# PSUM banks for attention's last transposes, and the queue that loads the gates' block sums

## The chip, the cores and the metric

The kernel runs on one core of a Trainium2 chip. The metric is device time in microseconds of one execution; the profile is one execution on the same core.

## The reference

One layer of a hybrid encoder over 1024 tokens and 16 learned meta tokens, width 1024. After an RMSNorm one input projection gives the operands of two branches and two gates. Branch A is neighbourhood attention (8 heads of 64, a window of 8 x 16 grid positions, meta keys always visible), branch Bm a bidirectional gated linear recurrence (HGRN2, 4 heads of 128). Then:

```
A = neighbourhood_attention(q, k, v, rpb) @ W_na_out ;  Bm = hgrn2(q, z_f, z_b, i, g) @ W_hg_out
h = h + (sigmoid(gate_na) * A + sigmoid(gate_hg) * Bm) @ W_o
h = h + relu(rmsnorm(h) @ W_up)^2 @ W_down ;  out = rmsnorm(h)
```

Matmuls keep float32 accuracy: each operand is split into a rounded high part and a low remainder, and a product is three matmuls, high by high, high by low and low by high.

## The kernel before

The stages follow each other: norm and transpose of the input, HGRN2 for four heads, attention for four pairs of heads, the gates, the branches' output projections, W_o, and the MLP. TensorE runs nearly all the time. Outside some stages that are recorded in written order, a scheduler sets each engine's order from the program; attention and the gates are such scheduled code, and it mixes the end of the first with the start of the second.

**Attention's end.** For each strip of 128 tokens and head, `scores` (two matmuls, L756 and L757) fills one of two PSUM banks of tag `s`; VectorE adds the bias and takes a minimum, ScalarE the exponential, VectorE scales (L766). `values`, two strips behind, transposes the probabilities on TensorE (L777, L779) into one of two banks of tag `t` (tile `ppt`), which ScalarE copies as the high part (L788) and VectorE turns into the low part (L789); both must have read a bank before it is filled again. Every fourth strip, a chain of matmuls (L793 to L802, tile `pov`) applies the values; VectorE moves the result to `OT` (L804, L806), and GpSimd's queue writes `OT` to DRAM (L817).

**The gates.** The 16 blocks of gate columns are computed in pairs by a scheme with sums of blocks (Winograd's). `first_gates` makes the first product of every pair for two pairs at a time: it loads two weight blocks of 512 KB through SyncE's queue (L102), splits them (ScalarE L112 into `hi`, VectorE L113 into `lo`) and runs chains of matmuls (L836 to L838) on two banks of tag `mm`; ScalarE copies the halves out (L869, L857). The `raw`, `hi` and `lo` tiles have two buffers each. The last call, for pairs 6 and 7, takes the last two blocks. Then `gate_pair` runs once per pair, with `second_operand` ahead of it: for each of four kinds of block sums of the activations, `t2`, `t1`, `t3`, `t4`, four tiles of 256 KB that `block_sums` had written to DRAM (`tsp`) in attention are loaded into `gv` (L889, five buffers, SyncE's queue) and split (ScalarE L96, VectorE L97). A `gv` buffer comes free when both have read it; the split tiles of `t3` stand where attention's `OT` stood, and wait for its write.

The engines and both kinds of queue take their work in order: a waiting instruction holds what stands behind it.

Of the kernel before, what the change touches and what calls it, by code (L numbers as in the profile page):

```python
# [26 lines left out]
NPAIR = 4  # L27
# [21 lines left out]
def layer(ctx: ExitStack, tc: tile.TileContext, x, meta, w_in, w_na, w_hg, w_o, w_up, w_dn,  # L49
          g_mix, g_mlp, g_fin, gain, bias, lbl, lmask, wmask, out):  # L50
    nc = tc.nc
    pe, act, dve, pool, sp = nc.tensor, nc.scalar, nc.vector, nc.gpsimd, nc.sync
# [20 lines left out]
    def bank(tag, name):  # L73
        return banks[tag].tile([P, 4, P], F32, tag=tag, name=name)
# [20 lines left out]
    def split(hi, lo, src):  # L95
        act.copy(hi, src)  # L96
        dve.tensor_tensor(lo, src, hi.bitcast(F32), op=ALU.subtract)  # L97
# [82 lines left out]
    tsp = {v: [dramp.tile([P, TH], F32, name=f"tsp_{v}_{k}") for k in range(4)] for v in ("t1", "t2", "t3", "t4")}  # L180
# [491 lines left out]
    with (tc.tile_pool(name="npr", bufs=1, side="right", reuse_waits="tile") as npr,  # L672
# [18 lines left out]
        for p in range(NPAIR):  # L691
# [43 lines left out]
            for b in (0, 4, 8):  # L735
                pt = bank("t", "vpt")
# [12 lines left out]
            def scores(s, i):  # L749
                js = [j for j in (s - 1, s, s + 1) if 0 <= j < 8]  # L750
                w = len(js) * SW
                o = 432 if s == 0 else 720 if s == 7 else 0
                sc = bank("s", "nsc").rearrange("p a b -> p (a b)")
                ksl = KS[i][:, js[0]:js[-1] + 1].rearrange("p s c -> p (s c)")
                kll = KL[i][:, js[0]:js[-1] + 1].rearrange("p s c -> p (s c)")
                pe.matmul(sc[:, :w], QX[i][:, s], ksl, start=True, stop=False)  # L756
                pe.matmul(sc[:, :w], QX[i][:, s], kll, start=False, stop=True)  # L757
                pr = npr.tile([P, 432], F32, tag="pr", name="pr", bufs=5)
                mn = npr.tile([P, 1], F32, tag="mn", name="mn", bufs=4)
                sm = npr.tile([P, 1], F32, tag="sm", name="sm", bufs=4)  # L760
                rc = npr.tile([P, 1], F32, tag="rc", name="rc", bufs=4)
                dve.tensor_tensor_reduce(out=pr[:, :w], in0=sc[:, :w], in1=NB[:, i, o:o + w], scale=1.0,  # L762
                                         scalar=3.0e38, op0=ALU.add, op1=ALU.min, accum_out=mn)
                act.activation(pr[:, :w], pr[:, :w], AF.Exp, bias=mn, scale=-1.0, accum_out=sm)
                dve.reciprocal(rc, sm)
                dve.tensor_scalar(pr[:, :w], pr[:, :w], rc, None, op0=ALU.mult)  # L766
                return js, pr

            def values(s, i, js, pr):
                g, e = divmod(s, 4)  # L770
                if e == 0:
                    po[i] = [npr.tile([P, 22, P], F32R, tag=f"PT{q}", name=f"PT{q}") for q in range(2)]
                PH, PL = po[i]
                m = len(js)
                pt = bank("t", "ppt")
                for k in range(m):
                    pe.transpose(pt[:, k], pr[:, k * SW:k * SW + P], ident)  # L777
                cen = js.index(s)
                pe.transpose(pt[:, m], pr[:, cen * SW + NM:cen * SW + NM + P], ident)  # L779

                b0 = 3 * (js[0] - 4 * g) + e + 3
                if s < 7:
                    runs = [(0, m + 1, b0)]
                else:
                    runs = [(0, m, b0), (m, 1, 4 * e + 9)]
                for k, n, b in runs:
                    hi = PH[:, b:b + 3 * n - 2:3]
                    act.copy(hi, pt[:, k:k + n])  # L788
                    dve.tensor_tensor(PL[:, b:b + 3 * n - 2:3], pt[:, k:k + n], hi.bitcast(F32), op=ALU.subtract)  # L789
                if e < 3:  # L790
                    return
                ov = bank("b", "pov")
                pe.matmul(ov, V[:, 8, i], PH[:, 9:22:4], start=True, stop=False)  # L793
                for a in range(-1, 5):
                    j = 4 * g + a
                    if 0 <= j < 8:
                        es = [q for q in range(4) if abs(a - q) <= 1]
                        e0, ne = es[0], len(es)
                        b = 3 * a + e0 + 3
                        pe.matmul(ov[:, e0:e0 + ne], V[:, j, i], PH[:, b:b + ne], start=False, stop=False)  # L800
                        pe.matmul(ov[:64, e0:e0 + ne], V[:, j, i, :64], PL[:, b:b + ne], start=False, stop=False)
                pe.matmul(ov, V[:, 8, i], PL[:, 9:22:4], start=False, stop=True)  # L802
                low = npr.tile([64, 4, P], F32, tag="low", name="low")
                dve.tensor_copy(low, ov[64:])  # L804
                dst = OT[64 * i:64 * i + 64].rearrange("p (r s c) -> p s r c", s=8, c=8)
                dve.tensor_tensor(dst[:, s - 3:s + 1], ov[:64].rearrange("p s (r c) -> p s r c", c=8),  # L806
                                  low.rearrange("p s (r c) -> p s r c", c=8), op=ALU.add)
# [3 lines left out]
            for st in steps:  # L811
                pend.append((*st, *scores(*st)))
                if len(pend) > 2:
                    values(*pend.pop(0))
            for st in pend:
                values(*st)
            pool.dma_start(osp[1][p], OT)  # L817


# [61 lines left out]
    def g_tile(tag, n, dt=F32, bufs=1):  # L881
        return gp.tile([P, n], dt, tag=tag, name=tag, bufs=bufs)

    def second_operand(v):
        for k in range(4):
            t = g_tile("gv", TH, bufs=5)
            if v not in aV:
                aV[v] = [gpr.tile([P, 4, TH], F32R, name=f"a{v}{q}") for q in range(2)]
            sp.dma_start(t, tsp[v][k])  # L889
            split(aV[v][0][:, k], aV[v][1][:, k], t)  # L890

    w_turn = [0]
# [55 lines left out]
    for v in ("t2", "t1", "t3", "t4"):  # L948
        second_operand(v)
# [28 lines left out]
    for br, wsrc in enumerate((w_hg, w_na)):  # L978
        for jj in range(0, KC, 2):
# [7 lines left out]
            for j in (jj, jj + 1):  # L987
                sg = sgp.tile([P, T], F32, tag="sg", name="sg")
                sp.dma_start(sg, gsp[8 * br + j])
                for h in range(2):  # L990
                    pm = mm_tile()
                    t = slice(h * TH, (h + 1) * TH)
# [614 lines left out]
```

## Time and profile before

| | us |
|---|---|
| runs shown | 1538.90, 1539.66, 1540.40 |
| their median | 1539.66 |
| profiled execution, its own time | 1541.84 |
| its span, from the first to the last instruction | 1540.0 |

The profiled execution lies 2.18 us above the median, and its span 1.84 us below its own time. TensorE is busy for 1504.0 us of the span, VectorE for 1029.9, ScalarE for 658.6, GpSimd for 377.9. Starts are given in us from the start of the span. "PE" is TensorE, "PEld" its weight loads, "DVE" VectorE, "ACT" ScalarE, "POOL" GpSimd, "SP" SyncE; a "q" behind an engine's name is its queue. A row's bracket tells how long the engine was idle ahead of it and what ended that.

### The profile page before, as it was taken

To read this page: it belongs to the slowest core of one execution; us is meant where nothing else is said; L and a number is where in the kernel's file an instruction comes from. 1 tells how busy PE (TensorE), PEld (TensorE's weight loads), DVE (VectorE), ACT (ScalarE), POOL (GpSimd) and SP (SyncE) were. 2 spreads that over 40 slices of the span, in tenths; PEclk is the share of its full clock that TensorE was granted. 3 is DMA by queue.
4 is the path that set the end of the run, shared out by engine and by line. 5 is a ranking of instruction groups with operands and counts; after the bars stand their busy time and mean duration, and the time that the engine had idled before them with its cause. 6 is when DMAs were issued, how large, how long until landed. Compare 5 with 4: busy or idle time off the path is not lost.

```text
span 1540.0 us, 23453 instructions
## 1 busy us (share of the span) xinstructions
PE 1504.0 (98%) x9192; PEld 1253.4 (81%) x9192; DVE 1029.9 (67%) x1603; ACT 658.6 (43%) x1175; POOL 377.9 (25%) x354
## 2 busy tenths in 40 slices
PE   7899999999999998999999999999999999999998
PEld 5788888888888887888888887888888888888886
DVE  6666666664966877666566358877777544877876
ACT  6231313124665667434223135555555533434444
POOL 2313131216225310011000122444333200232142
PEclk9999999999999999999999999999999999999999
DMA  4111111113123128434747123444444676563224
GB/s 168 43 29 56 29 56 29 56 29 120 58 72 120 49 76 260 143 123 158 252 158 246 42 83 129 158 153 154 151 151 153 202 270 235 194 232 115 96 82 151
DMA packets 142449, 195.61 MB, mean 127 GB/s; under 512 B 8049, under 2 KB 90097, under 8 KB 142338
## 3 DMA queue, kind: packets, MB, share of 16 engines
q1 hardware_dynamic: 133216, 172.53, 33.8%
q10 hardware_dynamic: 6946, 14.24, 2.4%
q0 software_dynamic: 2176, 7.34, 1.3%
q8 instruction: 72, 1.18, 0.3%
q14 instruction: 39, 0.32, 0.1%
HBM read 139.56 MB, written 54.53 MB: 126 GB/s over the span
## 4 chain that ended last, share of the span: by engine, by line
PE 89%; DVE 5%; issue 2%; ACT 2%; POOL 1%; DMA 1%; POOLq 0%; ACTq 0%; DVEq 0%
PE mm L122 11%; PE mm L123 11%; PE mm L124 10%; PE mm L1329 5%; PE pa L1329 4%; PE pb L836 4%; PE pb L838 4%; PE pb L837 4%; PE pb L1329 4%; PE pc L1329 4%; PE pc L838 3%; PE pc L836 3%; PE pc L837 3%; PE pa L838 2%; PE pa L837 2%
## 5 line engine op out<-in xcount | busy, mean ns | idle before, releaser
L122 PE MATMUL mm<-aT,hi 128*128 128x512 f32 (+2 forms) x640 | 230.6, 360 | 3.1 <-DVE QX L707 1.5
L124 PE MATMUL mm<-aT,lo 128*128 128x512 f32 (+2 forms) x640 | 227.8, 356 | 0.5 <-DVE lo L113 0.5
L123 PE MATMUL mm<-aT,hi 128*128 128x512 f32 (+2 forms) x640 | 226.4, 354 | 0.0
L122 PEld LDWEIGHTS mm<-aT,hi 128*128 128x128 f32 x640 | 121.8, 190 | 17.6 <-issue 1.7
L124 PEld LDWEIGHTS mm<-aT,lo 128*128 128x128 f32 x640 | 121.8, 190 | 14.2 <-DVE lo L113 1.0
L123 PEld LDWEIGHTS mm<-aT,hi 128*128 128x128 f32 x640 | 121.8, 190 | 12.3
L97 DVE TENSOR_TENSOR dl<-ur,dh 128x1024 fp32r<-128x1024 f32 x54 | 71.0, 1315 | 87.4 <-ACT dh L96 85.4
L96 ACT CAST dh<-ur 128x1024 fp32r<-128x1024 f32 x54 | 56.8, 1052 | 166.5 <-issue 91.2
L112 ACT CAST hi<-raw 128x1024 fp32r<-128x1024 f32 x36 | 37.8, 1051 | 99.1 <-PE mm L123 68.0
L1134 DVE TENSOR_TENSOR wl<-raw,wh 128x512 fp32r<-128x512 f32 x50 | 41.0, 822 | 36.5 <-ACT wh L1133 36.4
L1138 ACT ACTIVATE uv<-uv 128x512 f32<-128x512 f32 x48 | 30.4, 633 | 80.0 <-DVE uv L1246 48.9
L1134 DVE TENSOR_TENSOR wl<-sx,wh 128x512 fp32r<-128x512 f32 x70 | 61.0, 882 | 3.4 <-ACT wh L1133 3.3
L1133 ACT CAST wh<-sx 128x512 fp32r<-128x512 f32 x70 | 42.1, 619 | 42.2 <-PE pc L837 24.0
L1419 POOL TENSOR_TENSOR w<-w,tt 128x512 f32<-128x512 f32 x16 | 23.4, 1460 | 132.9 <-DVE tt L1418 113.2
L300 POOL TENSOR_TENSOR Y<-X,TN 128x512 f32<-128x512 f32 x20 | 34.2, 1711 | 86.1 <-DVE X L297 86.1
L113 DVE TENSOR_TENSOR lo<-raw,hi 128x1024 fp32r<-128x1024 f32 x36 | 46.5, 1293 | 9.6 <-ACT hi L112 9.5
L762 DVE CUSTOM_DVE_ANT_0 pr<-nsc,NB 128x432 f32<-128x432 f32 (+1 forms) x64 | 35.2, 559 | 26.6 <-PE nsc L757 26.4
L836 PE MATMUL pb<-nt,wh 128*128 128x512 f32 x128 | 50.2, 392 | 0.4 <-DVE uv L1216 0.2
L122 PE MATMUL mm<-wh,mT 128*128 128x512 f32 x128 | 50.2, 392 | 0.0
L837 PE MATMUL pb<-nt,wh 128*128 128x512 f32 x128 | 49.9, 390 | 0.0
L838 PE MATMUL pb<-nt,wl 128*128 128x512 f32 x128 | 49.9, 390 | 0.0
L124 PE MATMUL mm<-wh,mT 128*128 128x512 f32 x128 | 49.9, 390 | 0.0
(391 smaller groups left out, 4354.0 us busy)
## 6 DMA issues: line engine op xcount, KB each, us to landing
raw<-in_w_in SPq DMA_DIRECT2D x56, 512.0 KB, 3.9
ur<-usp SPq DMA_DIRECT2D x54, 512.0 KB, 3.4
raw<-in_w_up SPq DMA_DIRECT2D x16, 1024.0 KB, 6.1
usp<-us SPq DMA_DIRECT2D x60, 256.0 KB, 2.2
sg<-gsp SPq DMA_DIRECT2D x16, 512.0 KB, 3.3
w<-in_w_dn SPq DMA_DIRECT2D x16, 512.0 KB, 4.5
usp<-uv SPq DMA_DIRECT2D x30, 256.0 KB, 3.5
gsp<-gv ACTq DMA_DIRECT2D x24, 256.0 KB, 2.5
```

The source lines that it names most:

```text
L96: act.copy(hi, src)
L97: dve.tensor_tensor(lo, src, hi.bitcast(F32), op=ALU.subtract)
L113: dve.tensor_tensor(lo[:, :kc], raw[:, :kc], hi[:, :kc].bitcast(F32), op=ALU.subtract)
L122: pe.matmul(ps, lh, rh, start=first, stop=False)
L123: pe.matmul(ps, lh, rl, start=False, stop=False)
L124: pe.matmul(ps, ll, rh, start=False, stop=last)
L836: pe.matmul(ps, lhs[0][:, c], rhs[0][:, k], start=first and k == 0, stop=False, skip_group_check=True)
L837: pe.matmul(ps, lhs[0][:, c], rhs[1][:, k], start=False, stop=False, skip_group_check=True)
L838: pe.matmul(ps, lhs[1][:, c], rhs[0][:, k], start=False, stop=k == 3, skip_group_check=True)
L1133: act.copy(v(hi), src)
L1134: dve.tensor_tensor(v(lo), src, v(hi).bitcast(F32), op=ALU.subtract)
L1329: pe.matmul(ps, a[n == 2][:, q, j * P:(j + 1) * P], b[n == 1][:, q], start=first and n == 0, stop=last and n == 2, skip_group_check=True)
```

## The change

In the last pair of heads the last two strips' transposes go to a bank of tag `s` (the scores' banks, which nothing needs by then) rather than `t`. And of the 16 loads of block sums, the twelve of `t1`, `t3` and `t4` are issued by GpSimd's queue rather than by SyncE's; the four of `t2` stay. With a blank line added, line numbers from 815 on are one higher after the change.

```diff
-            def values(s, i, js, pr):
+            def values(s, i, js, pr, tag="t"):
...
-                pt = bank("t", "ppt")
+                pt = bank(tag, "ppt")
...
+
             for st in pend:
-                values(*st)
+                values(*st, *(["s"] if p == NPAIR - 1 else []))
...
-            sp.dma_start(t, tsp[v][k])
+            (sp if v == "t2" else pool).dma_start(t, tsp[v][k])
```

The scheduler then puts the instructions of this stretch in another order. On TensorE, at the end of attention, before (`ppt_6570`, `ppt_6588`, `ppt_6595`, `ppt_6602` are the last four strips' transposes, `mm_...` products of `first_gates`; the chain `pov_6541` stands just ahead of the first row):

```order
L777 MATMUL ppt_6588<-ident_77,pr_6525 128x128 x3
L779 MATMUL ppt_6588<-ident_77,pr_6525 128x128
L777 MATMUL ppt_6595<-ident_77,pr_6560 128x128 x3
L779 MATMUL ppt_6595<-ident_77,pr_6560 128x128
L836 MATMUL mm_6746<-aT00_87,hi_6728 128x512
L777 MATMUL ppt_6602<-ident_77,pr_6580 128x128 x2
L779 MATMUL ppt_6602<-ident_77,pr_6580 128x128
L837 MATMUL mm_6746<-aT01_88,hi_6728 128x512
L836 MATMUL mm_6732<-aT00_87,hi_6722 128x512
```

And after, from the same place on:

```order
L777 MATMUL ppt_6588<-ident_77,pr_6525 128x128 x3
L779 MATMUL ppt_6588<-ident_77,pr_6525 128x128
L777 MATMUL ppt_6595<-ident_77,pr_6560 128x128 x2
L779 MATMUL ppt_6595<-ident_77,pr_6560 128x128
L777 MATMUL ppt_6602<-ident_77,pr_6580 128x128 x2
L779 MATMUL ppt_6602<-ident_77,pr_6580 128x128
L837 MATMUL mm_6746<-aT00_87,hi_6728 128x512
L838 MATMUL mm_6746<-aT01_88,hi_6728 128x512
L837 MATMUL mm_6732<-aT00_87,hi_6722 128x512
L838 MATMUL mm_6732<-aT01_88,hi_6722 128x512
L839 MATMUL mm_6732<-aT00_87,lo_6723 128x512
L837 MATMUL mm_6732<-aT00_87,hi_6722 128x512
L793 MATMUL pov_6610<-PT0_6568,Vn_3965 128x512
```

One transpose of `ppt_6595` has gone ahead of the chain `pov_6541`, the last strips' transposes stand together, and the chain `pov_6610` comes after six products of `mm_...` where before it came after twelve. On ScalarE all high parts of the transposes (L788) now stand ahead of the cast of the weight block `hi_6728`, where before two of them stood behind it.

On ScalarE, around the cast of the weight block `hi_6868` (the first of pairs 6 and 7), before (`at30` and `at40` are the split tiles of `t3` and `t4`, `go` and `g1` results of `first_gates`):

```order
L96 CAST at30_6993<-gv_6992 128x512
L869 COPY g1_5_6631<-mm_6822 128x512
L96 CAST at30_6993<-gv_6998 128x512
L96 CAST at30_6993<-gv_7002 128x512
L96 CAST at30_6993<-gv_7006 128x512
L857 ACTIVATE go_6848<-mm_6808 128x512
L112 CAST hi_6868<-raw_6866 128x1024
```

And after:

```order
L96 CAST at30_6993<-gv_6992 128x512
L96 CAST at30_6993<-gv_6998 128x512
L870 COPY g1_5_6631<-mm_6822 128x512
L96 CAST at30_6993<-gv_7002 128x512
L96 CAST at30_6993<-gv_7006 128x512
L96 CAST at40_7011<-gv_7010 128x512
L858 ACTIVATE go_6848<-mm_6808 128x512
L112 CAST hi_6868<-raw_6866 128x1024
```

A ninth load, the first of `t4` (`gv_7010`), has come ahead of the cast of `hi_6868`, and the second of `t3` ahead of the copy `g1_5`.

On GpSimd's queue, after (before, the write of `OT`, `osp_3`, followed the first row directly, and the next instruction was the first of the gates' pairs):

```order
L192 DMA tsp_t_3_132<-rt 128x512
L890 DMA gv<-tsp_t_0_117 128x512
L818 DMA osp_3_100<-OT 128x1024
L890 DMA gv<-tsp_t_1_118 128x512
L890 DMA gv<-tsp_t_2_119 128x512
L890 DMA gv<-tsp_t_3_120 128x512
L890 DMA gv<-tsp_t_0_125 128x512
L890 DMA gv<-tsp_t_1_126 128x512
L890 DMA gv<-tsp_t_2_127 128x512
L890 DMA gv<-tsp_t_3_128 128x512
L890 DMA gv<-tsp_t_0_129 128x512
```

Eleven loads now stand behind the write of `OT`, three more of `t4` after the last row; on SyncE's queue the weight blocks follow each other without loads between them.

## Rows read from the trace of the kernel before

**Rows 1.** The page: busy time by engine, and the chain that ended last, by engine.

```profile
PE 1504.0 (98%) x9192; PEld 1253.4 (81%) x9192; DVE 1029.9 (67%) x1603; ACT 658.6 (43%) x1175; POOL 377.9 (25%) x354
...
PE 89%; DVE 5%; issue 2%; ACT 2%; POOL 1%; DMA 1%; POOLq 0%; ACTq 0%; DVEq 0%
```

**Rows 2.** Who waited for whom between 575 and 640 us: engine and line that waited, what ended it, us in total, times, longest.

```profile
ACT at L96 <- DMA gv<-tsp_t: 3.1, 1, 3.1
...
PE ppt L777 <- DVE PT L789: 2.3, 1, 2.3
...
PE mm L836 <- ACT hi L112: 1.9, 1, 1.9
```

**Rows 3.** TensorE's instructions at the end of attention: start, length in us, line, tiles.

```profile
584.97 0.27 PE L779 MATMUL ppt<-ident,pr 128*128 128x128 f32 x1
587.59 0.52 PE L777 MATMUL ppt<-ident,pr 128*128 128x128 f32 x3 [2.35 <-DVE PT L789]
...
588.86 0.39 PE L836 MATMUL mm<-aT,hi 128*128 128x512 f32 x1
589.09 0.39 PE L837 MATMUL mm<-aT,hi 128*128 128x512 f32 x1
...
591.17 0.39 PE L793 MATMUL pov<-PT,Vn 128*128 128x512 f32 x1
...
592.96 0.39 PE L836 MATMUL mm<-aT,hi 128*128 128x512 f32 x1
```

**Rows 4.** ScalarE's instructions in the same stretch.

```profile
585.28 0.58 ACT L788 CAST PT<-ppt 128x512 fp32r<-128x512 f32 x1 [0.20 <-PE ppt L779]
...
585.76 1.05 ACT L112 CAST hi<-raw 128x1024 fp32r<-128x1024 f32 x1
586.71 0.59 ACT L869 COPY g<-mm 128x512 f32<-128x512 f32 x1
588.26 0.93 ACT L788 CAST PT<-ppt 128x512 fp32r<-128x512 f32 x2 [0.96 <-PE ppt L779]
589.09 1.66 ACT L96 CAST aT<-gv 128x512 fp32r<-128x512 f32 x3
```

**Rows 5.** VectorE's instructions in the same stretch and later; the last row ends with the split of the last load of `t1`.

```profile
584.85 0.69 DVE L804 COPY low<-pov 64x512 f32<-64x512 f32 x1 [1.56 <-PE pov L802]
...
586.77 1.27 DVE L789 TENSOR_TENSOR PT<-ppt,PT 128x512 fp32r<-128x512 f32 x2
...
589.10 1.00 DVE L789 TENSOR_TENSOR PT<-ppt,PT 128x512 fp32r<-128x512 f32 x2
...
595.20 0.68 DVE L806 TENSOR_TENSOR OT<-pov,low 64x512 f32<-64x512 f32 x1
595.91 1.29 DVE L97 TENSOR_TENSOR aT<-gv,aT 128x512 fp32r<-128x512 f32 x2
...
602.48 1.29 DVE L97 TENSOR_TENSOR at<-gv,at 128x512 fp32r<-128x512 f32 x2 [0.44 <-ACT at L96]
```

**Rows 6.** TensorE's instructions at the last two weight blocks of `first_gates`.

```profile
609.08 0.39 PE L838 MATMUL mm<-aT,lo 128*128 128x512 f32 x1
611.35 0.50 PE L836 MATMUL mm<-aT,hi 128*128 128x512 f32 x1 [1.88 <-ACT hi L112]
...
612.61 0.50 PE L838 MATMUL mm<-aT,lo 128*128 128x512 f32 x1 [0.53 <-DVE lo L113]
```

**Rows 7.** ScalarE's instructions ahead of them.

```profile
607.95 1.92 ACT L96 CAST at<-gv 128x512 fp32r<-128x512 f32 x3 [3.07 <-DMA gv<-tsp_t]
609.77 0.59 ACT L857 ACTIVATE go<-mm 128x512 f32<-128x512 f32 x1
610.26 1.03 ACT L112 CAST hi<-raw 128x1024 fp32r<-128x1024 f32 x1
```

**Rows 8.** The issues on the queues: SyncE's (start, us from the first issue to the end of the last, count) and GpSimd's, then the first load of the second SyncE row alone, with its own length (ns).

```profile
592.77 4.83 SPq L889 DMA_DIRECT2D gv<-tsp_t  x4
...
601.47 8.84 SPq L889 DMA_DIRECT2D gv<-tsp_t  x7
...
596.18 0.54 POOL L817 DMA_DIRECT2D osp<-OT  x1 [50.70 <-DVE OT L806]
...
L889 SPq DMA_DIRECT2D gv<-tsp_t x1: 2126/2126/2126, 601.5 to 601.5; - x1
```

**Rows 9.** Stretches: us, busy time of the engines (instructions), granted clock, mean busy share of the DMA engines, GB/s.

```profile
596.00:602.00 6.00, 6.00 (x28) 4.99 (x27) 4.82 (x6) 4.45 (x8) 0.54 (x1) 1.00 0.92 288
602.00:608.00 6.00, 6.00 (x28) 4.95 (x28) 2.03 (x4) 2.13 (x5) 0.00 (x0) 1.00 1.06 359
```

**Rows 10.** DMA queues between 598 and 600 us: packets, MB, share of the 16 engines (q0 is GpSimd's, here the write of `OT`; q1 SyncE's).

```profile
q0 software_dynamic: 99, 0.38, 70.7%
q1 hardware_dynamic: 104, 0.21, 28.5%
```

**Rows 11.** Time from issue to landing (min/median/max of the DMAs in a stretch): the two weight blocks issued at 598.4 and 600.7 us; the five loads issued from 601.5 to 605.2; the last two, from 609.3; and GpSimd's four writes of block sums from 534.7 to 544.9 us with the length of their issues in ns.

```profile
DMA to landing us min/median/max: 6.6/6.7/6.8
...
DMA to landing us min/median/max: 4.9/5.2/6.5
...
DMA to landing us min/median/max: 2.6/3.2/3.8
...
L192 POOL DMA_DIRECT2D tsp_t<-rt x4: 562/564/584, 534.7 to 544.9; - x4
```

## The prediction

> **What bounds the kernel now.** I read the page first. TensorE is busy for 1504.0 of 1540.0 us, and 89% of the chain that ended last is its own [rows 1]; the reader is to see that an edit of queues and banks can pay only where TensorE stands still. So I looked next for what moves: the program's order differs between about 575 and 640 us alone, and the waits of that stretch, sorted by who waited, come second [rows 2]. Two of TensorE's waits count: one at the transposes and one at the products of `first_gates`. Third I read the instructions around both places in order of time, on each engine that waits or is waited for, and last the issues and the DMA queues behind the second.
>
> **Place A, attention's last transposes.** TensorE idles for 2.35 us before 587.59, until VectorE's L789 has read a `t` bank [rows 3]. VectorE is late because L789 stands behind L804 and what follows it, from 584.85; L789 begins at 586.77 [rows 5].
>
> **Place B, the last weight blocks.** TensorE begins a product at 609.08, idles 1.88 us for ScalarE's `hi`, does one product, and idles 0.53 for VectorE's `lo`, whose product begins at 612.61 [rows 6]. Products follow each other at 0.23 us (588.86 to 589.09 [rows 3]), so the product of 612.61 was due at 609.08 + 3 x 0.23 = 609.77, and 2.84 us are lost. ScalarE was late because it had waited 3.07 us for a block sum, then cast three of them from 607.95, copied at 609.77 and only then began `hi` at 610.26 [rows 7]. The load it waited for was issued at 601.47, where the issue itself took 2.13 us [rows 8], and landed 6.5 us after it was issued [rows 11].
>
> **The change, part 1: the bank.** The wait of 2.35 us goes. What is late next is `hi_6728` on ScalarE, since two more casts of transposes stand ahead of it. Casts of that kind cost 0.48 (585.28 to 585.76) and two together 0.83 (588.26 to 589.09) [rows 4]. In before the cast of `hi` began at 585.76, behind the first; in the change it begins at 585.76 + 0.83 = 586.6, or 586.7 with the transpose put ahead of the chain, and with its 1.05 ends at about 587.75. The transposes left (0.52 for three [rows 3]) are done well before that, so TensorE gives 2.35 back only down to 587.8. Two products take it to 588.3; in before that place (its first product at 588.86, the transposes done) was reached at 588.86, so some 0.55 us are won. Then the chain `pov_6610` stands behind six products rather than twelve, and it needs the last low part. VectorE's first L789 would still end its turn no earlier than 586.77 plus half of 1.27, and three more of about 0.6 and the last transposes' remainder of 0.4 put that at about 589.2, where TensorE arrives at 588.3 + 4 x 0.23 = 589.2; a cast of some 0.2 has to follow, and costs it. The chain takes 592.96 - 591.17 = 1.79 [rows 3], to about 591.2; six products fewer have been done by then, 6 x 0.23 = 1.4, so the place of 592.96 is reached at 592.6. Net: **0.3 us won at A**; bounds 0 (VectorE's low parts later by 0.3) and 2.35 (`hi` in time).
>
> It is then lost again: TensorE reaches B 0.3 us earlier and waits 0.3 us longer for the same `hi`, unless part 2 makes `hi` earlier. All between is rows of TensorE at work: 6.00 of 6.00 us in both stretches from 596 to 608 [rows 9].
>
> **Part 2: twelve loads on GpSimd's queue.** SyncE is rid of twelve issues; the longest cost 2.13 us and held what followed. On GpSimd's queue the first load goes early. Behind it stands the write of `OT`, which waits for L806 on VectorE (595.20, 0.68 us long) and went out at 596.18 [rows 5, 8]; the eleven other loads wait with it, where SyncE issued four from 592.77 on [rows 8]. The scheduler lets two subtractions (1.29 for both [rows 5]) change places with L806, which could put the write 1.3 us later or 0.3 earlier. An issue on GpSimd's queue takes 0.54 to 0.56 us [rows 8, 11], so eleven cost 6 us, beside SyncE's 4.83 for four and 8.84 for seven; no issue is the bound. A buffer is: `t4`'s first load needs that of `t1`'s last, read by VectorE at 602.48 + 1.29 = 603.77 [rows 5], say 603.5 with A's gain.
>
> The bytes stay the same, and the DMA engines are full there: busy share 0.92 and 1.06 from 596 to 608 us [rows 9]. So the change cannot make transfers faster in sum; it can only put the loads ahead of the weight blocks, or behind them. The load of `t4` now has to land before `hi_6868` is cast, since its cast has come ahead of it. From issue to landing the five loads of before took 4.9 to 6.5 us, median 5.2 [rows 11]. The 6.5 was the one at 601.47, straight behind two weight blocks; `t4`'s is issued later than that, and I take 4.9. It lands at 603.5 + 4.9 = 608.4. Then a cast of 1.92 / 3 = 0.64, the copy's 0.49 (609.77 to 610.26), and `hi` begins at 609.5 rather than 610.26 [rows 7]: **0.8 us won at B**. Ends: 3.2 us to landing (the last two loads, median [rows 11]) gives 606.7 and 2.4 won; 6.7 (as the weight blocks) with the write of `OT` 1.0 later gives 611.2 and 2.0 lost. The point that decides is a landing at 609.2.
>
> The Trainium skill, "DMA: Bandwidth & Descriptors", section "Queues, rings and completion order", says that each DMA engine takes turns between the queues it has work for, packet by packet. With the large packets on GpSimd's queue and small ones on SyncE's (between 598 and 600 us: 99 packets for 0.38 MB against 104 for 0.21 MB [rows 10]) turns by packet favour GpSimd's loads. By that rule alone the sum would be that of the first rival.
>
> After B all is rows of TensorE again, and the gain or loss there is passed on whole. **Sum: 0.8 us won**, A's part inside it. The profiled execution's own 1541.84 becomes 1541.0; it stands 2.18 above the median of the runs, 1539.66, and against that I forecast 1538.9.
>
> **Rivals.**
>
> 1. *GpSimd's loads outrun the weight blocks.* For it: with both queues at work, the write of `OT` had 70.7% of the engines and SyncE's queue 28.5% [rows 10]; and SyncE's weight blocks are no longer held by a 2.13 us issue. Against: the same bytes through full engines, and weight blocks that then land later themselves. Loads would land by 606.7 or earlier, ScalarE never waits, and B closes: 2.4 won, or up to 2.84 + 0.3 = 3.1. Time 1537.3 to 1536.5. Chance 0.20.
>
> 2. *The loads stand behind the write of `OT`* (slower). One queue now takes the write (0.5 MB) and eleven loads in order, while the weight blocks have SyncE's queue to themselves. For it: four loads that were issued from 592.77 now wait till 596, and the ninth must land before `hi`. Against: the transfers of 592.77 to 597.6 were early, and ScalarE's waits came at 605 to 608 only [rows 7]. It decides from a landing of `t4`'s first load after 609.2, and each us behind costs one: at 611.2, 2.0 lost, 1541.7; the middle is 1540.9. Chance 0.22.
>
> 3. *Nothing comes of it.* A's gain is swallowed, and the load lands within 0.2 us of 609.2. For it: the wait moves from one load to the next in the same full engines. 1539.7. Chance 0.12.
>
> 4. *GpSimd's issues are held up by VectorE.* If each of the eleven took what the longest issue of SyncE took, 2.13 us [rows 8], rather than 0.54, the ninth load would be issued at about 596.2 + 8 x 2.13 = 613.2 and land 4.9 later at 618; 8.9 us lost, 1548.6. Against: the issue at 596.18 took 0.54 us while VectorE was in its two-input subtractions from 595.91 to 597.20, and four others 0.56 to 0.58 [rows 5, 8, 11]. Chance 0.03. The Trainium skill, "DMA: Bandwidth & Descriptors", section "SWDGE vs HWDGE vs iDMA", speaks against this change: GpSimd writes the descriptors of its DMAs to rings in SBUF, and VectorE in a two-port mode locks it out of there, while queues such as SyncE's are immune. By that rule the trace shows no delay so far, at the one issue that lies in such a subtraction.
>
> **How the numbers follow.** Forecast (0.2 to 1.9 won) 0.43, rivals 0.20, 0.22, 0.12, 0.03. The range holds 8 in 10 if it leaves out rival 4, the far end of rival 2 and the far end of rival 1: **1536.7 to 1541.0**. A measurement of this kernel can tell some 0.2%, 3.1 us, from no change. Faster by more needs all of rival 1 and something beyond: 0.10. Slower by more is rival 4 and a late end of rival 2: 0.05. Within: 0.85.
>
> **What would show it.** Right at A: TensorE's idle time before the transposes is gone and a shorter one, some 1 to 2 us, stands before a product and is ended by ScalarE's L112. Right at B: `hi` of the last pairs begins near 609.2 to 609.5 and TensorE's wait for it is about 1.3 to 1.5 us, while ScalarE's longest wait is for a load of `t3` or `t4`. Rival 1 shows as no wait of TensorE at B and ScalarE busy there; rival 2 as one of over 2.2 us, with landings on GpSimd's queue after 609; rival 4 as issues above 1 us on GpSimd. Wrong altogether would be a difference of several us outside 575 to 640 us, or stretches before 575 us that are no longer the same.

## The result, and the profile after

The change made the kernel slower: 1544.71 us in the median of 17 runs (1541.16 to 1546.84), beside 1540.21 for the kernel before in 17 runs (1538.90 to 1543.23). The ratio is 1.0022, with a 95% interval of 1.0015 to 1.0029, so some 3.4 us. The forecast was 1538.9, in a range of 1536.7 to 1541.0. The profiled execution of the changed kernel took 1544.73 us, with a span of 1542.9.

The page of the changed kernel, busy time by engine and chain by engine, answers to [rows 1]: TensorE has the same instructions and is busy 1.6 us longer, and 2.9 us have been added to the span.

```profile
PE 1505.6 (98%) x9192; PEld 1253.4 (81%) x9192; DVE 1032.3 (67%) x1603; ACT 659.2 (43%) x1175; POOL 384.5 (25%) x366
...
PE 87%; DVE 6%; issue 2%; ACT 2%; DMA 2%; POOL 1%; SPq 0%; POOLq 0%; ACTq 0%; DVEq 0%
```

TensorE's waits of the changed kernel from 575 to 740 us (line that waited, what ended it, us in total, times, longest) answer to [rows 2]. The wait for L789 is gone as forecast, and a wait for `hi` stands in its place, beside the one at B that before had too (the first row counts both). The second row is new, and it is not in the stretch that the prediction looked at.

```profile
PE mm L837 <- ACT hi L112: 3.8, 2, 2.1
PE pb L837 <- DVE gv L930: 1.4, 1, 1.4
PE mm L839 <- DVE lo L113: 0.5, 1, 0.5
PE pov L793 <- ACT PT L788: 0.3, 1, 0.3
```

TensorE's instructions of the changed kernel at places A and B (start, length, line, tiles, idle time before) answer to [rows 3, 6]:

```profile
586.78 0.50 PE L837 MATMUL mm<-aT,hi 128*128 128x512 f32 x1 [1.73 <-ACT hi L112]
...
588.73 0.50 PE L793 MATMUL pov<-PT,Vn 128*128 128x512 f32 x1 [0.27 <-ACT PT L788]
...
610.98 0.50 PE L837 MATMUL mm<-aT,hi 128*128 128x512 f32 x1 [2.05 <-ACT hi L112]
611.32 0.39 PE L838 MATMUL mm<-aT,hi 128*128 128x512 f32 x1
612.24 0.65 PE L839 MATMUL mm<-aT,lo 128*128 128x512 f32 x1 [0.53 <-DVE lo L113]
612.69 0.63 PE L837 MATMUL mm<-aT,hi 128*128 128x512 f32 x1
613.12 0.63 PE L838 MATMUL mm<-aT,hi 128*128 128x512 f32 x1
...
615.67 0.48 PE L838 MATMUL mm<-aT,hi 128*128 128x512 f32 x1
615.99 0.39 PE L839 MATMUL mm<-aT,lo 128*128 128x512 f32 x1
616.22 0.40 PE L837 MATMUL mm<-aT,hi 128*128 128x512 f32 x1
```

The issues on GpSimd's queue and ScalarE's cast of `hi` for place B answer to [rows 7, 8]; the first load of `t4` is the first of the last pair of issues, at 603.95:

```profile
577.73 0.55 POOL L890 DMA_DIRECT2D gv<-tsp_t  x1 [33.16 <-DVE mn L762]
594.38 0.54 POOL L818 DMA_DIRECT2D osp<-OT  x1 [16.10 <-DVE OT L806]
595.35 2.34 POOL L890 DMA_DIRECT2D gv<-tsp_t  x4 [0.43 <-issue]
...
603.95 1.15 POOL L890 DMA_DIRECT2D gv<-tsp_t  x2 [0.47 <-DVE at L97]
```

```profile
609.89 1.03 ACT L112 CAST hi<-raw 128x1024 fp32r<-128x1024 f32 x1
```

In TensorE's rows above, the reader is to see the distance between starts. After the stop at B products follow each other at 0.43 us (612.69 to 613.12), and from 615.99 on again at 0.23: for 3.4 us TensorE runs at half speed. The table by stretch says the same in its column of the granted clock (us, busy time of the engines, clock, share of the DMA engines, GB/s):

```profile
606.00:611.00 5.00, 2.95 (x13) 2.11 (x13) 2.18 (x5) 3.37 (x6) 1.09 (x2) 1.00 0.85 310
611.00:616.00 5.00, 4.47 (x12) 3.22 (x13) 3.61 (x4) 2.40 (x4) 0.00 (x0) 0.66 0.74 222
616.00:640.00 24.00, 24.00 (x107) 19.86 (x106) 13.32 (x18) 8.52 (x13) 1.61 (x1) 1.00 0.39 119
700.00:730.00 30.00, 28.62 (x127) 23.38 (x126) 19.58 (x23) 13.24 (x17) 2.90 (x2) 1.00 0.48 160
```

The Trainium skill, "TensorE: Matmul & The Clock Gate", section "Part 1: The HAM clock gate (the "warmup" mystery)", says that TensorE falls to half its clock after an idle window of some 3.4 us, and that the windows run freely. The length and the pace here agree; the idle time does not, since TensorE stood still here for 2.05 and then for 0.53 us only.

To add up where time went, the same product is looked up in two traces, and the difference of its starts is taken, less that difference at 575 us (the profiles are there between 4.2 us ahead of before's and 0.8 behind, whatever the kernel). In steps, with the sum at 800 us and the time of the runs against before's of the same chip beside it:

| kernel | 575 to 606 (A and after) | the stop at B | to 620 (clock) | near 727 | at 800 | runs: ratio to before |
|---|---|---|---|---|---|---|
| change | 0.0 | +0.5 | +1.6 | +1.3 | +3.5 | 1.0022 |
| change again | +1.3 | +0.7 | +1.5 | +1.6 | +5.2 | 1.0026 |
| before again | 0.0 | -0.6 | 0.0 | +0.2 | -0.4 | 0.9999 |
| bank alone | -0.1 | +0.2 | 0.0 | +0.3 | +0.4 | 0.9997 |
| queue alone | +4.0 | -1.6 | -0.1 | +1.5 | +3.8 | 1.0019 |

A row is one execution; each ratio is over 11 to 17 runs. In the row of the queue alone the half clock came at place A, for 6.8 us, and stands in the first column. The two executions of before differ by 0.6 us at B.

### The profile page after: what moved, and what is told of

Same layout as the page of the kernel before. It is cut to its first block, busy times and chain, and to the rows that moved or that the text cites. A ratio compares the mean times of both kernels' runs of the same rounds, so it can differ in the third digit from the quotient of the medians.

```text
span 1542.9 us, 23448 instructions
## 1 busy us (share of the span) xinstructions
PE 1505.6 (98%) x9192; PEld 1253.4 (81%) x9192; DVE 1032.3 (67%) x1603; ACT 659.2 (43%) x1175; POOL 384.5 (25%) x366
## 4 chain that ended last, share of the span: by engine, by line
PE 87%; DVE 6%; issue 2%; ACT 2%; DMA 2%; POOL 1%; SPq 0%; POOLq 0%; ACTq 0%; DVEq 0%
PE mm L122 11%; PE mm L123 11%; PE mm L124 10%; PE mm L1330 5%; PE pa L1330 4%; PE pb L837 4%; PE pb L839 4%; PE pb L838 4%; PE pc L1330 4%; PE pb L1330 4%; PE pc L839 3%; PE pc L837 3%; PE pc L838 3%; PE pa L839 2%; PE pa L837 2%
## 5 line engine op out<-in xcount | busy, mean ns | idle before, releaser
L97 DVE TENSOR_TENSOR dl<-ur,dh 128x1024 fp32r<-128x1024 f32 x54 | 71.0, 1315 | 87.3 <-ACT dh L96 87.1
```

## The experiments

Four theories in the end: **clock** (a stop at B or A costs 3.4 us of half speed; theory 1 in the expectations), **first load** (the one load that goes early on GpSimd's queue delays a weight block; theory C), **meeting** (a wait near 727 us that two subtractions near 718 us decide; theory 3 at first, then A and A2), and **late loads** (the loads of `t1` stand behind the write of `OT`; theory E).

**Each part alone, and both kernels again.** The edits are the two halves of the diff: `values(*st, "s")` alone, and `(sp if v == "t2" else pool)` alone.

> The bank of the last transposes alone; all loads stay on SyncE's queue. Theory 1 (the clock): a longer stop of TensorE at the last weight blocks halves its clock for some 3.4 us, which costs 1.6 us; since the bank lets TensorE arrive 0.3 us earlier and `hi` comes no sooner, the stop grows to about 2.2 us and over, and this kernel shows a granted clock near 0.5 for 3.4 us after 611 and is 1 to 2 us slower than before. Theory 2 (the queue): the loss is all from GpSimd's loads, so this one is within 0.5 us of before, with the clock at 1.00. Theory 3 (the wait at 727 us, a late load in the gate pairs): it comes with any shift in time, whichever part makes it; 1.3 us slower with no change of the clock.

> The twelve loads on GpSimd's queue alone; the transposes keep their banks. Theory 1: TensorE's order is that of before, it arrives at the last weight blocks as in before and `hi` comes 0.4 us earlier, so the stop is about 1.5 us, the clock stays at 1.00, and it is 0 to 0.8 us faster. Theory 2: the loads are what costs; 2 to 3.5 us slower. Theory 3: 1.3 us slower with a wait of TensorE near 727 us and the clock at 1.00.

> The changed kernel again, unchanged, for a second profile. Theory 1: the granted clock is again near 0.6 for about 3.4 us after the stop at 611, and 3.4 us slower than before. Theory 3: TensorE waits over 1 us near 729 us again. If one of the two is missing while the time is the same, the missing one is not the cause.

> The kernel before, unchanged, for a second profile and for the spread. All theories: ratio 1.000 within 0.001; theory 1: the clock stays at 1.00 between 600 and 640 us, in most executions; theory 3: no wait of TensorE near 727 us.

Measured: bank 0.9997 (0.9988 to 1.0006), queue 1.0019 (1.0011 to 1.0028), change again 1.0026 (1.0017 to 1.0035), before again 0.9999 (0.9990 to 1.0008). So the loss is the queue's, and the bank is worth nothing that can be told. My theory 1 had the bank's stop at B grow to 2.2 us; it was 1.38 us, with the clock up. It also had the queue alone at full clock; there the half clock came at place A, from 586.43 on, within a stop of 3.76 us. That kernel's table by stretch:

```profile
585.00:590.00 5.00, 2.21 (x9) 2.06 (x10) 4.17 (x6) 1.68 (x4) 0.00 (x0) 0.64 0.65 250
590.00:595.00 5.00, 5.00 (x19) 4.02 (x19) 4.63 (x8) 3.54 (x7) 0.55 (x1) 0.67 0.51 147
```

And VectorE there, just ahead (to be read beside [rows 5]):

```profile
583.63 0.69 DVE L804 COPY low<-pov 64x512 f32<-64x512 f32 x1 [1.56 <-PE pov L802]
585.64 0.69 DVE L826 TENSOR_TENSOR sx<-raw 128x512 f32<-128x512 f32 x1 [1.32 <-DMA raw<-in_w_in]
586.36 0.68 DVE L806 TENSOR_TENSOR OT<-pov,low 64x512 f32<-64x512 f32 x1
586.97 1.27 DVE L789 TENSOR_TENSOR PT<-ppt,PT 128x512 fp32r<-128x512 f32 x2
```

L826 waits 1.32 us for a weight block (`raw` of `gate_sums`, L910), and L789, for which TensorE's transposes wait, stands behind it. In before that block came in time, and L826 followed L804 directly:

```profile
585.46 0.68 DVE L826 TENSOR_TENSOR sx<-raw 128x512 f32<-128x512 f32 x1
```

All three profiles with the queue have two more things in common: the wait near 727 us (1.4 to 1.7 us; 0 to 0.4 in the others), and a stop of half clock somewhere.

**Where the wait near 727 us comes from.** Around 717 us of the changed kernel, engines but TensorE:

```profile
717.10 0.69 DVE L935 TENSOR_TENSOR gv<-pb,g 128x512 f32<-128x512 f32 x1 [1.12 <-PE pb L839]
717.38 0.62 ACT L96 CAST hi<-raw 128x512 fp32r<-128x512 f32 x1 [0.73 <-PE pb L839]
717.92 1.29 POOL L936 TENSOR_TENSOR gv<-gv,p 128x512 f32<-128x512 f32 x1 [11.99 <-DVE gv L935]
718.04 1.72 DVE L97 TENSOR_TENSOR lo<-raw,hi 128x512 fp32r<-128x512 f32 x1 [0.25 <-ACT hi L96]
...
719.68 0.68 DVE L937 TENSOR_TENSOR gv<-gv,pc 128x512 f32<-128x512 f32 x1
719.79 0.32 SPq L975 DMA_DIRECT2D raw<-osp  x1
```

And the same place in before:

```profile
715.68 0.62 ACT L96 CAST hi<-raw 128x512 fp32r<-128x512 f32 x1 [0.45 <-PE pb L837]
715.84 0.69 DVE L934 TENSOR_TENSOR gv<-pb,g 128x512 f32<-128x512 f32 x1 [1.28 <-PE pb L838]
716.45 0.68 DVE L97 TENSOR_TENSOR lo<-raw,hi 128x512 fp32r<-128x512 f32 x1
716.66 1.62 POOL L935 TENSOR_TENSOR gv<-gv,p 128x512 f32<-128x512 f32 x1 [11.99 <-DVE gv L934]
717.16 0.32 SPq L974 DMA_DIRECT2D raw<-osp  x1
```

The subtraction of VectorE (L97) and that of GpSimd meet. Whichever starts first runs at its pace (0.68 on VectorE, 1.29 on GpSimd), and the other is held (1.62 on GpSimd, 1.72 on VectorE). Where VectorE is second, SyncE's next load goes out 4.4 us after the last rather than 3.2, and TensorE waits 1.4 us at 729 for what follows. What decides is ScalarE's cast: it begins 0.16 us ahead of VectorE's L934 in before, and 0.28 us behind the same addition (L935) in the changed kernel. Over 14 profiles without an edit of this subtraction: up to 0.12 us behind, the wait was 0 to 0.5 us (9 of 9); from 0.27 us on, 1.4 to 1.8 (5 of 5).

Why is the cast late? By counting ScalarE's instructions in the trace, there is a pause of 0.28 us in front of the 832nd in the changed kernel, which is this cast; in before one stands in front of the 704th, 128 earlier, near 604 us. The change takes four of ScalarE's waits away ahead of the place, and so would move every later instruction by four against these pauses, if they come once in 128. The next experiment puts four instructions back.

```diff
-        act.copy(p3, pc)
+        act.copy(p3, pc); idle = gpr.tile([P, 1], F32, name=f"idle{m}") if m == 3 else None; [act.copy(idle, p3[:, :1]) for _ in range(4 * (m == 3))]
```

> The changed kernel with four copies of one column added on ScalarE in the fourth gate pair, some 70 us ahead of the place, so that ScalarE's stream of instructions is as long there as in the kernel before (four waits were lost by the change). Theory A (a stop of 0.28 us every 128 instructions of ScalarE): in the changed kernel the stop falls on the last small cast near 717 us, delays VectorE into GpSimd's subtraction and ends in TensorE's wait of 1.4 to 1.7 us near 727 to 729; here it falls on an instruction that waits anyway, VectorE's subtraction there takes 0.68 rather than 1.72 us, and the wait at 727 is at most 0.4: 1.3 us faster than the changed kernel, ratio to before 1.0014 or less. Theory B (the later time or the other queue itself makes the wait): nothing changes, wait of 1.4 to 1.7, ratio 1.0022 to 1.0026.

Its ratio was 1.0027 (1.0014 to 1.0040). The wait near 727 was gone, and 2.1 us were lost elsewhere: products from 620 to 726 us each took longer, in steps of 0.1 us in every 24, with no wait and the clock at 1.00. I put this down to the four bytes a partition of the new tile, which move what is allocated behind it; that step is argued, not shown. So the test was spoiled, and so was this one, which shared the tile:

```diff
-            (sp if v == "t2" else pool).dma_start(t, tsp[v][k])
+            (sp if v == "t2" or (v == "t1" and k == 0) else pool).dma_start(t, tsp[v][k])
```

> Both: first load of `t1` on SyncE's queue, and four copies on ScalarE; the transposes in the scores' banks and eleven loads on GpSimd's queue as in the change. Theories A and C together: no wait near 727 over 0.4 us, no wait of VectorE for the weight block, and a ratio to before of 0.999 to 1.0007; if one of them is wrong the ratio is 1.001 or more.

It came out at 1.0028 (1.0018 to 1.0039), with the same slow products. Again, with the copies made in place (`act.copy(p3[:, :1], p3[:, :1])`):

> The changed kernel with four copies of one column onto itself on ScalarE in the fourth gate pair: the run before it with four copies had a new tile, and its products between 620 and 735 us each took 2% longer (0.1 us in every 24). Here no tile is added. Theory A (the stop every 128 instructions of ScalarE): no wait of TensorE over 0.5 us near 727, products at 0.227 us as in before, so 1.3 us faster than the changed kernel, ratio to before 1.0014 to 1.0018. Theory B (later time or other queue): wait of 1.4 to 1.7 us, ratio 1.0022 to 1.0026.

1.0012 (1.0003 to 1.0021), 0.3 us near 727, products at 0.227 us: theory A held there. The clock stayed up in this profile too, which theory A has no part in.

**The first load.** With the edit of the diff above, and no copies:

> The changed kernel with the first load of `t1` on SyncE's queue again (last of its five loads there, issued near 583), the other eleven on GpSimd's. Theory C (the early load holds up the weight block for the gates' sums): that block lands about 4.9 to 5.0 us after its issue as in before, not 5.8 to 7.1, VectorE's first sum does not wait for it, and the stops of TensorE at attention's end shrink by up to 1.4 us: 0.5 to 1.5 us faster than the changed kernel; the wait near 727 stays. Theory D (the block is late because of the eleven other loads or of chance): no change at that place, ratio 1.0022 to 1.0026.

And the reverse, before with this one load on GpSimd's queue:

> The kernel before with one edit: the first load of `t1` on GpSimd's queue, the rest on SyncE's. Theory C (this load, issued 5.6 us earlier, holds up the weight block for the gates' sums): the block lands 5.8 to 7.1 us after its issue rather than 4.9, VectorE's first sum waits for it, TensorE's stop at the transposes is 2.6 to 3.8 us rather than 2.4: 0.3 to 1.4 us slower, and up to 3 where the clock drops after it; and since two waits of ScalarE go with this edit, theory A adds its 1.4 us near 727: ratio 1.001 to 1.002. Otherwise 1.000.

The time from issue to landing of the weight block (min/median/max of the one load), in the changed kernel's second profile, then with the first load on SyncE's queue, then in before with it alone on GpSimd's:

```profile
DMA to landing us min/median/max: 7.1/7.1/7.1
```

```profile
DMA to landing us min/median/max: 4.9/4.9/4.9
```

```profile
DMA to landing us min/median/max: 6.5/6.5/6.5
```

The times were 1.0017 (1.0009 to 1.0026) and 1.0009 (1.0001 to 1.0018): the block's delay is shown both ways. Over all 20 profiles the block landed 4.7 to 5.3 us after its issue with this load on SyncE's queue (12 of 12) and 5.8 to 7.1 with it on GpSimd's (8 of 8). With the bank of the change, TensorE behind A stood 0.3 us ahead of before in the ten profiles with the load on SyncE's queue, and between level and 1.3 us late in the six others, which are 1.0 us later in the mean. In before with this load alone on GpSimd's queue, TensorE's stop at the transposes was 3.44 us rather than 2.35, and 3.4 us of half clock followed (granted clock 0.57 from 588 to 592 us); of the 2.7 us lost there, 1.4 came back at B, where the stop for `hi` was 0.45 us only. Theory A's wait near 727 did not come in that kernel (0.3 us); the cast was early there though two waits had gone.

**The clock, and all together.**

```diff
+            if m == 6:
+                spare = up_bank("pa")
+                for _ in range(7):
+                    pe.matmul(spare, aV["b11"][0][:, 0, :P], aV["b11"][0][:, 0], start=True, stop=True)
             chain(ps[-1], b[0], aV["b11"], True)
```

> The changed kernel with seven products (1.6 us) into a PSUM bank that nothing reads, placed right ahead of the first product of the last two weight blocks, where TensorE stands still for 2 us. Theory 1 (the clock halves after a stop there): the clock is 1.00 from 606 to 640 us, and the kernel is up to 1.6 us faster than the changed one in those executions in which that one is throttled, on average perhaps 1 us: ratio 1.0015 to 1.002. If the clock drops after the stop although the stop is filled, or the clock stays up and the time does not fall, theory 1 is wrong or its share is small.

> The changed kernel with all three causes taken away that the profiles name: first load of `t1` on SyncE's queue, seven products in the stop at the last weight blocks, four copies in place on ScalarE. If these are the whole loss but for a `hi` that is 0.7 us late: ratio to before 1.000 to 1.0008, with the clock at 1.00 between 575 and 640 us and no wait over 0.5 us near 727. If the ratio is 1.0015 or more, a cause is missing.

The seven products alone: 1.0025 (1.0014 to 1.0037), clock 1.00, not faster. By what was expected of it, that speaks against the clock, or for a small share; with six runs it can't say more. All three edits: 1.0013 (1.0005 to 1.0022), and the wait near 727 was back at 1.8 us: the cast came 0.35 us behind without any pause, ScalarE being late for other reasons. Copies that shift instructions were the wrong tool; the meeting itself had to go:

```diff
-        pool.tensor_tensor(u3, u3, p3, op=ALU.subtract)
+        (dve if m == 6 else pool).tensor_tensor(u3, u3, p3, op=ALU.subtract)
```

> The changed kernel with one GpSimd subtraction (of the seventh gate pair, L935, the one near 718 us) given to VectorE, where it takes about 0.7 us instead of 1.3 to 1.6 and cannot meet another on the shared way to SBUF. Theory A2 (the wait near 727 comes from which of the two subtractions, VectorE's or GpSimd's, starts first): no wait over 0.5 us near 727 whatever is late, 1.3 us faster than the changed kernel: ratio to before 1.0013 to 1.0018. Rival: the wait comes from the loads near 720 alone and stays 1.3 or more: ratio 1.0022 or more.

> The run above with the first load of `t1` on SyncE's queue again. Theory C: the weight block for the gates' sums lands 4.9 to 5.3 us after its issue, TensorE does not wait for the last low part at attention's end, another 0.7 to 1.3 us faster: ratio 1.0003 to 1.001. If the first load's share is nothing in the mean: 1.0013 to 1.0018 as above.

> The run above with the seven products in the stop at the last weight blocks. Theory 1 (half clock for 3.4 us in part of the executions, 1.6 us each time): the clock is 1.00 from 575 to 640, and it is 0.3 to 1.2 us faster than the run above, ratio 0.9997 to 1.0005, with less spread between the runs; if the clock rarely drops without the first load's delay, no difference.

> The bank of the last transposes with all loads on SyncE's queue, and that subtraction on VectorE: the candidate to beat both kernels. Before has only 0 to 0.4 us of wait near 727 and the bank gains 0.3 us that is lost again at the last weight blocks: ratio to before 0.999 to 1.000, so likely not to be told from it.

| the changed kernel with | ratio | 95% interval |
|---|---|---|
| nothing (first measurement, second) | 1.0022, 1.0026 | 1.0015 to 1.0029, 1.0017 to 1.0035 |
| the subtraction on VectorE | 1.0017 | 1.0009 to 1.0026 |
| and the first load on SyncE's queue | 1.0011 | 1.0003 to 1.0020 |
| and seven products in the stop | 1.0002 | 0.9993 to 1.0010 |

VectorE in the first of these, where GpSimd's subtraction now follows on VectorE (L935, 0.68 us) and L97 is not held:

```profile
719.24 0.69 DVE L97 TENSOR_TENSOR lo<-raw,hi 128x512 fp32r<-128x512 f32 x1
719.84 0.68 DVE L935 TENSOR_TENSOR gv<-gv,p 128x512 f32<-128x512 f32 x1
```

The clock at B in the second, and in the third:

```profile
611.00:616.00 5.00, 3.11 (x9) 2.20 (x10) 4.13 (x5) 3.78 (x6) 0.00 (x0) 0.82 0.69 208
616.00:621.00 5.00, 5.00 (x20) 4.04 (x19) 1.75 (x4) 1.56 (x3) 0.00 (x0) 0.84 0.57 164
```

```profile
606.00:611.00 5.00, 4.62 (x19) 3.49 (x19) 2.43 (x4) 3.05 (x6) 1.09 (x2) 1.00 0.71 267
611.00:616.00 5.00, 3.98 (x16) 2.99 (x17) 4.26 (x5) 4.02 (x7) 0.00 (x0) 1.00 0.86 250
```

Each step was about as large as its theory had it. Neighbouring intervals overlap; it is the order of the steps, and the rows, that carry this.

That 1.0002 does not mean that nothing is left of the change's cost, since the products also help a kernel with all loads on SyncE's queue: the next section has one at 0.9989 with the same subtraction and six products. Beside that one, 1.0002 is still some 2.0 us slower (an estimate, from two chips). Nor do the executions as a whole show that the change loses more clock than before. The mean granted clock was 0.9956 over 141 runs of before, 0.9955 over 28 of the change, and 0.9967 over 50 of the five kernels with products (each figure is over the whole execution, with its other stretches of half clock). So the clock's 1.6 us is real in the profiles that have it, but how much of the change's loss against before it makes is open.

The bank alone with that subtraction on VectorE was 1.0003 (0.9994 to 1.0011), and its profile had the half clock at B, too, behind a stop of 1.75 us: the half clock does not need GpSimd's queue, and a stop there is a risk in every version. Over 13 profiles with an unfilled stop at B of over 1.2 us (counting the wait for `hi` alone): none of the three up to 1.52 us was followed by half clock, and seven of the ten from 1.66 to 2.35. None of the five with products in it was.

**A version that beats both, and the late loads.** Both kernels have the subtraction on VectorE and products in the stop; the first has all loads on SyncE's queue and six products, the second `t1` there and `t3`, `t4` on GpSimd's, with seven.

> The bank of the last transposes, all sixteen loads on SyncE's queue, the subtraction near 718 on VectorE, and six products in the stop at the last weight blocks. The run without the products lost 1.4 us to the half clock in its profile; with them the clock is 1.00 from 575 to 640 us, and 0.3 to 0.9 us are won against before: ratio 0.9994 to 0.9998, likely not to be told from no change. If the clock drops all the same, theory 1 is in doubt.

> As the run with the products and the first load on SyncE's queue, but all four loads of `t1` there; `t3` and `t4` on GpSimd's. Theory E (the loads of `t1` behind the write of OT make `hi` of the last weight blocks late): TensorE reaches the product after that stop 0.5 us or more earlier than that run, and the ratio to before is 0.9993 to 1.000. Theory F (loads on GpSimd's queue are slower themselves): as that run, 1.0002 or more, and slower than the run on SyncE's queue alone.

An earlier try of the second, without those two edits but with the copies in place:

> The changed kernel with all four loads of `t1` on SyncE's queue again (eight loads on GpSimd's), and the four copies in place. Theory E (the loads of `t1` stand behind the write of `OT`, which makes every later load of the five buffers late, and `hi` with them): `hi` of the last weight blocks comes 0.7 to 1.5 us earlier than in the changed kernel, TensorE's stop there is 1.5 us or less, the clock stays up: ratio to before 0.999 to 1.000. Theory F (the loads of `t3` and `t4` on GpSimd's queue are slower themselves): the stop is 2 us as in the changed kernel, ratio 1.0008 to 1.0018.

The first: 0.9989 (0.9980 to 0.9999), median 1539.50 beside 1540.94 of before on the same chip, so some 1.7 us faster than before and, by the ratios, 5 faster than the change; more than the 0.3 to 0.9 that were expected. Its clock was 1.00 from 575 to 640 us. Its TensorE waits from 575 to 740 us have no third cause:

```profile
PE mm L836 <- ACT hi L112: 2.1, 2, 1.7
PE mm L838 <- DVE lo L113: 0.5, 1, 0.5
```

The second: 1.0005 (0.9996 to 1.0014), the earlier try 1.0008 (0.9999 to 1.0018). Against before, TensorE loses 0.34 us over the stop at B in the second, and 0.92 with three of the loads of `t1` behind the write of `OT`: theory E holds in the trace. All profiles with the bank agree: over the stop at B they lose 0.5 to 1.0 us with those loads behind the write (11 of 11), and -0.1 to 0.3 with all of `t1` on SyncE's queue (5 of 5). Theory E doesn't hold in the time, which is no better than 1.0002 and meets what theory F (loads on GpSimd's queue are slower themselves) had of it. What eight loads on GpSimd's queue still cost beside SyncE's (1.0005 against 0.9989) is in neither profile, whose TensorE stands level at 1530 us, counted from 575. That stays open.

## Why the prediction was wrong

- **Part 1, the bank: right.** The wait for L789 went, `hi` became what is late, TensorE stood 1.73 us for it until 586.78 (forecast 587.8; this execution was 0.9 us ahead at 575). The gain of 0.25 us went to the chain's wait for its last cast (0.27) in the change, and was lost again by B in the bank alone. Alone: no difference that can be told.
- **"It lands at 603.5 + 4.9 = 608.4": the 603.5 was wrong, the 4.9 right, and 0.8 us won at B became 0.5 lost.** `t4`'s first load went out at 603.95 and landed at 608.86, 4.9 us later; `hi` began at 609.89, and its product at 610.98, 0.37 us earlier than in before. That looks near the forecast, but this execution was 0.9 us ahead at 575. Counted as before counts, the load went out at 604.9 rather than 603.5, `hi` began at 610.8 rather than 609.5, and TensorE left B 0.5 us late. Rival 2 had the sign and the place: the write of `OT` went out at 594.38, four loads behind it at 595.35, and those of before from 592.77 on [rows 8]. The loads of `t1` in that group were read late, and `t4`'s load waits for the buffer of the last.
- **"On GpSimd's queue the first load goes early": the cost of this was not counted.** Going 5.3 us ahead (577.73 against 583.05; 4.4 counted from 575), it delays the weight block that VectorE's sum needs, and the sum stands ahead of L806 and L789. A's lower bound of 0 was wrong: with the queue A cost up to 1.3 us, and more where the clock dropped. Part 2 put nothing at this term.
- **"After B all is rows of TensorE again, and the gain or loss there is passed on whole": wrong twice.** At half clock rows of TensorE are longer, and a stop of 2 us can bring that (1.5 and 1.6 us in the two profiles of the change; what it makes against before is open). And in before VectorE's L929 ended at 726.70, and the product near 727 that waits for it began at 726.75, so there was no slack at all; the chain of before passes through there. The meeting of two subtractions cost 1.3 to 1.7 us. Neither was a rival.
- **Rival 4 was rightly put at little:** each of the twelve issues of loads on GpSimd's queue took 0.55 us.
- **The range** was built from rivals at A and B alone. Of the 3.7 us by which the result lies above it, 0.55 come from before itself, whose median was 1540.21 over 17 runs and 1539.66 over the three shown. From 1.0024, the mean of the two measurements, the steps' ratios give 1.1 us for the meeting, 0.9 for the first load, 1.4 for the stop and 0.3 left over, each uncertain by more than 1 us. The 1.4 is a gain that before's queue order has as well, so it is no price of the change. The traces put the change's own prices at about 1.0 us for the first load, 0.5 to 1.0 at B for the late loads and 1.3 to 1.7 for the meeting, less 0.3 for the bank; the profile that lost no clock at B, the change with seven products, was 3.2 us late at 800.

The Trainium skill, "DMA: Bandwidth & Descriptors", section "Issuing engines are not separate DMA queues", says that DMAs from several engines run on the same 16 DMA engines and that a second issuer saves the time on the sequencer only. That rule, which the prediction did not use, speaks against this change, and the runs bear it out: the early load put 0.26 MB beside a weight block that was due, and the block landed 1 to 2 us later.

## What to carry to other kernels

A load that is moved earlier is paid by what it then overlaps with: look for the next transfer on the full engines and for who waits for that. A stop of TensorE of about 2 us should be counted with a chance of half clock behind it (here seven profiles of ten); with products that nobody reads put into it, no profile of five had that, though the time fell with them in two comparisons and not in a third. Where an edit changes only timing, look along the whole chain behind it for places without slack, and for pairs of VectorE and GpSimd instructions that start within some 0.3 us of each other: their order can turn.

## What the runs showed that I had not expected

- Half clock for 3.4 us came with stops of 1.66 to 2.35 us for `hi`, in six of seven cases followed by one of 0.53 for `lo` two products later. The Trainium skill, "TensorE: Matmul & The Clock Gate", section "Why this matters for your kernels", advises against idle gaps over some 3 us; here less was enough in seven of ten.
- VectorE's float32 subtraction of 128 x 512 took 0.68 us alone and 1.47 to 1.74 behind a GpSimd one that had begun; GpSimd's took 1.28 when it began first and 1.61 to 1.79 behind VectorE's. The Trainium skill, "GPSIMD Engine Reference", section "8. Key points", names this sharing; the price is from these rows.
- With a new tile of four bytes a partition, products from 620 to 726 us were 2% longer (0.232 rather than 0.227 us), 2.1 us in all; without the tile they were not. Why is not shown.
- ScalarE paused for 0.28 us ahead of its 704th instruction in before and of its 832nd in the change. That such a pause comes once in 128 instructions is inferred from these places; at others of that count none can be seen (before, at the 1600th).
